# Queries and keys of the undilated pattern: from attention's projection stream to block products beside the values

## The chip, the cores and the metric

The kernel runs on one core of a Trainium2 chip. The metric is the device time of one execution in microseconds, lower is better. TensorE (PE) multiplies, VectorE (DVE) and ScalarE (ACT) do arithmetic on tiles, GpSimd (POOL) does a little arithmetic and issues some DMAs, and SyncE (SP) issues the others. Each engine works its own instructions off in order and waits at an instruction until that instruction's inputs and buffers are there.

## The reference, cut to what matters

Two residual layers on 1024 tokens of width 1024: a gated token mixer with its MLP, then attention with its MLP. Every input and weight is f32. Attention mixes three patterns (window, dilation); each has its own q, k and v for 16 heads of 64, all out of one matrix `b_w_qkv` of 1024 rows and 9 x 1024 columns.

```python
B_PATTERNS = ((128, 1), (512, 4), (2048, 16))

def mixer_b(h, w_qkv, w_out, slopes):
    B, S, _ = h.shape
    qkv = (h @ w_qkv).reshape(B, S, N_PAT, 3, B_HEADS, B_HEAD_DIM)
    outs, lses = [], []
    for g, (window, dilation) in enumerate(B_PATTERNS):
        o, lse = dilated_branch(qkv[:, :, g, 0], qkv[:, :, g, 1], qkv[:, :, g, 2],
                                window, dilation, slopes)
        outs.append(o)
        lses.append(lse)
    wts = jax.nn.softmax(jnp.stack(lses, axis=0), axis=0)[..., None]
    o = jnp.sum(wts * jnp.stack(outs, axis=0), axis=0)
    return o.reshape(B, S, B_HEADS * B_HEAD_DIM).astype(h.dtype) @ w_out
```

`dilated_branch` computes, within blocks, scaled scores plus a bias that falls with distance, a causal window mask, softmax and the weighted sum of v; it returns the log of the sum too, by which the patterns are mixed.

## The kernel before

**Split numbers.** A matrix is kept as a high part in a fast f32 format (ACT's cast, line 102) and the low rest (DVE's difference, line 103). A product is three matmuls: high by high, high by low, low by high.

**Block products.** The large matrix products of the MLPs and of v are made from half-size blocks: seven products of 512 by 512 blocks instead of eight, with sums and differences of blocks prepared beforehand. In `values` the steps are `V_STEPS`, for each pattern the products 1, 2, 5, 6, 7, 4, 3. One product is four row tiles `m` of twelve matmuls (line 1248). `RightForms` loads and prepares the weight blocks two steps ahead, `second` builds the forms of the tokens, `evict` empties an accumulator: products 1, 5 and 6 are only kept (line 1218), the others are completed (line 1222), split and stored to DRAM by a DMA that POOL issues (line 1228), from one of two buffers `vs`.

**Attention.** Work is in 24 groups, one for each of 8 head pairs and 3 patterns, in the order 2, 1, 0 of `order` (line 1312). A group has 8 slots, 4 per head, of two positions each; functions are put in slots with `at`. For tile pair `m` of a head: `scores` (two matmuls per tile, then DVE adds the bias and takes the maximum, line 1422, and ACT takes exponentials, line 1424); `transposes` one slot and a half after the scores `when` they are complete (PE into PSUM, then split by ACT and DVE); and `weighted`, one and a half slots later (PE, line 1470). POOL makes each head's bias tile (line 1404). PSUM has two banks each for scores, weighted sums, projections and transposes.

**The projection stream.** q and k of every group come from `project`, a generator: 24 groups x q and k x 2 halves x 8 steps of three matmuls (line 1344). Forty steps run ahead of slot 0 and two after each position, twelve matmuls a slot. A unit of weights is loaded one unit ahead and split (line 353, then 102 and 103); each half's accumulator is split into q or k per head, and POOL copies q's high part to the other 64 partitions (line 1354), since a score is one product over 128 rows (q high twice, against k high and low) and one with q low.

**What else is in the slots.** `load_v` loads a group's v for both heads four slots ahead. `statistics`, and in `merge` the functions `read`, `factors`, `spread`, `scale` and `add`, mix the three patterns of a head pair under the slots of the next pair; maxima, sums and factors go through DRAM. In slots 2 to 27 eight rows of the residual pass through POOL (`affine_load`, `affine_row`, lines 1596 to 1602), pinned to program order on POOL's queue. In the last group's slots the output projection (`ending`, line 389) takes the place of the stream.

**What sets the order.** The program is written in the order of the slots. A planner in the compiler may move an instruction forward on its engine where it reckons its inputs ready and its buffer free, unless `keep_in_program_order` pins it. A tile of a pool with `bufs` buffers under a tag waits until the tile that had its buffer is done with.

## Time and profile before

| | |
|---|---|
| median of 3 runs | 2761.18 us (2759.01 to 2768.53) |
| profiled execution | 2765.4 us, its span 2763.7 us |
| granted TensorE clock, mean | 0.994 |
| value stage, first to last block matmul | 999.1 to 1233.2 us |
| attention, first projection to last weighted sum | 1233.4 to 2057.9 us |
| projection matmuls in attention (line 1344) | 2304 |
| block matmuls of v (line 1248) | 1008 |

The span runs from the first to the last instruction of the profiled execution, and its own time is that of the same execution. Busy time is a union over an engine's instructions; matmuls follow each other before the one ahead has ended, so their mean duration is longer than what one adds to the total. The idle time of an engine is put down to what ended it.

### The profile page before, as it was taken

The page shows a single profiled execution, that of the slowest core. Times are in us where ns is not written, and L with a number is a line of the kernel's source. Part 1 is how long each engine was busy: PE and PEld are TensorE (multiplying, and loading weights), DVE is VectorE, ACT ScalarE, POOL GpSimd, SP SyncE. Part 2 cuts the span into 40 slices and gives each one's busy share as a digit, 9 for nine tenths or more (in the row PEclk, how much of TensorE's full clock was granted, in tenths as well). Part 3 has the DMA queues.
Part 4 walks back from the last instruction along what each step waited for, and adds up shares of the span by engine and source line. Part 5 has one row for each costly group of instructions (what it writes and reads, how often), then busy time and mean ns, then how long its engine had stood idle before and what let it go on. Part 6 is the DMA issues. An engine that isn't in the chain of part 4 may idle for free.

```text
span 2763.7 us, 36368 instructions
## 1 busy us (share of the span) xinstructions
PE 2684.8 (97%) x12954; PEld 2231.6 (81%) x12954; DVE 2022.2 (73%) x3616; ACT 1417.7 (51%) x2651; POOL 211.1 (8%) x213
## 2 busy tenths in 40 slices
PE   6999999999999999999999999999999999999998
PEld 5787787887888878888888888888877788878887
DVE  6787698787877788555677667667669965568887
ACT  3354475555443464445566665666564755544432
POOL 1001000000000001113510100111120000000000
PEclk9999999999999999999999999999999999999999
DMA  7543346667946545544533323323334564485562
GB/s 260 162 129 115 116 140 217 222 216 260 329 132 191 190 152 196 193 162 144 150 89 90 97 71 94 93 82 98 100 101 156 183 207 145 153 306 193 175 203 88
DMA packets 318187, 441.82 MB, mean 160 GB/s; under 512 B 49148, under 2 KB 174500, under 8 KB 318004
## 3 DMA queue, kind: packets, MB, share of 16 engines
q1 hardware_dynamic: 308500, 404.87, 46.3%
q0 software_dynamic: 9504, 34.61, 3.3%
q8 instruction: 102, 1.67, 0.3%
q14 instruction: 81, 0.66, 0.1%
HBM read 330.27 MB, written 109.13 MB: 159 GB/s over the span
## 4 chain that ended last, share of the span: by engine, by line
PE 69%; DVE 15%; DMA 7%; ACT 4%; issue 3%; POOL 1%; SPq 0%; DVEq 0%; ACTq 0%; POOLq 0%
PE psd L955 22%; PE psk L1344 7%; PE psua L796 7%; PE psv L1248 7%; PE psq L1344 6%; PE psuc L796 3%; DMA adaw<-in_ada_w_dram 3%; PE psd_wout L389 2%; PE pv L1470 2%; PE psu L368 2%; PE psd_wo L389 2%; PE psv L470 2%; DVE adaacc L128 2%; PE psub L796 1%; DVE left L103 1%
## 5 line engine op out<-in xcount | busy, mean ns | idle before, releaser
L796 PE MATMUL psua<-right,left 128*128 128x512 f32 x1536 | 365.8, 392 | 0.1
L955 PE MATMUL psd<-rhi,lhi 128*128 128x512 f32 x896 | 350.4, 391 | 3.0 <-ACT part L827 3.0
L955 PE MATMUL psd<-rlo,lhi 128*128 128x512 f32 x896 | 350.2, 391 | 0.2
L955 PE MATMUL psd<-rhi,llo 128*128 128x512 f32 x896 | 350.0, 391 | 0.0
L796 PEld LDWEIGHTS psua<-right,left 128*128 128x128 f32 x1536 | 288.8, 189 | 61.9 <-DVE right L103 1.0
L1424 ACT ACTIVATE p<-p,stat 128x128 f32<-128x128 f32 (+1 forms) x384 | 171.3, 446 | 168.4 <-DVE stat L1422 156.3
L955 PEld LDWEIGHTS psd<-rhi,lhi 128*128 128x128 f32 x896 | 169.0, 189 | 39.8 <-ACT part L827 3.9
L955 PEld LDWEIGHTS psd<-rlo,lhi 128*128 128x128 f32 x896 | 168.9, 188 | 35.7 <-DVE rlo L103 1.1
L955 PEld LDWEIGHTS psd<-rhi,llo 128*128 128x128 f32 x896 | 168.9, 189 | 35.2
L796 PE MATMUL psuc<-right,left 128*128 128x512 f32 x768 | 187.8, 391 | 0.0
L1344 PE MATMUL psk<-form_L,wk_hi 128*128 128x512 f32 x576 | 185.0, 402 | 0.0
L1344 PE MATMUL psq<-form_L,wq_hi 128*128 128x512 f32 x576 | 184.8, 402 | 0.0
L103 DVE TENSOR_TENSOR pTlo<-pT,pThi 128x512 fp32r<-128x512 f32 (+1 forms) x160 | 99.5, 623 | 107.9 <-ACT pThi L102 107.1
L128 DVE SCALAR_TENSOR_TENSOR adaacc<-adaw,silu_c,adaacc 128x512 f32<-128x512 f32 x168 | 132.7, 800 | 57.9 <-DMA adaw<-in_ada_w_dram 57.0
L796 PEld LDWEIGHTS psuc<-right,left 128*128 128x128 f32 x768 | 143.5, 188 | 30.1 <-DVE right L103 0.5
L103 DVE TENSOR_TENSOR left<-ws,left 128x512 fp32r<-128x512 f32 x128 | 87.8, 687 | 72.9 <-ACT left L102 71.1
L103 DVE TENSOR_TENSOR llo<-lraw,lhi 128x1024 fp32r<-128x1024 f32 x112 | 136.3, 1217 | 0.8 <-ACT lhi L102 0.8
L1422 DVE CUSTOM_DVE_ANT_0 p<-sc,bias 128x128 f32<-128x128 f32 (+1 forms) x384 | 122.5, 346 | 13.0 <-POOL bias L1404 7.6
L102 ACT CAST left<-ws 128x512 fp32r<-128x512 f32 x128 | 79.1, 620 | 98.4 <-DVE ws L717 88.3
L102 ACT CAST rhi<-rraw 128x1024 fp32r<-128x1024 f32 x48 | 50.6, 1054 | 142.9 <-issue 113.6
L1248 PE MATMUL psv<-vrhi,form_S 128*128 128x512 f32 x384 | 119.8, 390 | 1.2 <-DVE vpart L1222 0.7
L102 ACT CAST lhi<-lraw 128x1024 fp32r<-128x1024 f32 x112 | 117.3, 1047 | 3.4 <-PE psua L796 3.4
(299 smaller groups left out, 6277.6 us busy)
## 6 DMA issues: line engine op xcount, KB each, us to landing
lraw<-forms SPq DMA_DIRECT2D x112, 512.0 KB
adaw<-in_ada_w_dram SPq DMA_DIRECT2D x192, 256.0 KB
up<-in_mlp_w_up_dram SPq DMA_DIRECT2D x64, 512.0 KB
forms<-s SPq DMA_DIRECT2D x128, 256.0 KB
rraw<-in_mlp_w_down_dram SPq DMA_DIRECT2D x64, 512.0 KB
forms<-part SPq DMA_DIRECT2D x96, 256.0 KB
v<-vs POOLq DMA_DIRECT2D x48, 512.0 KB, 3.7
v<-v SPq DMA_DIRECT2D x32, 512.0 KB
```

The lines of the kernel that those rows point to most:

```text
L102: first = A.copy(hi, src) if hi_engine is A else hi_engine.tensor_copy(hi, src)
L103: return first, lo_engine.tensor_tensor(lo, src, hi, op=ALU.subtract)
L128: ins = V.scalar_tensor_tensor(acc[:], raw[:], silu_c[:, k : k + 1], acc[:], ALU.mult, ALU.add)
L368: T.matmul(dst, s[a], m[b], start=(n == 0), stop=(n == last))
L389: T.matmul(p[:], stat[a][:, k, o : o + P], u[b][:, w], start=n == 0, stop=n == count - 1)
L470: T.matmul(sums[u, half][:], units[u][a_][:, k * P : (k + 1) * P], hT[half][b_][:, k, :], start=k == 0 and a_ + b_ == 0, stop=k == KD - 1 ...
L796: T.matmul(acc, w[:, a, k, :], right[p][:, b, k, :], start=p in (1, 2, 5) and k + a + b == 0, stop=k == 3 and a == 1, skip_group_check=True)
L955: ins = T.matmul(sums[kind, m][:], l[a][:, k, m * P : (m + 1) * P], r[b][:, k, :], start=p in (1, 5, 2, 3) and kp + k + a + b == 0, stop=k ...
L1248: T.matmul(acc, left[:, a, 2 * kp + k, m * P : (m + 1) * P], r[b][:, k, :], start=p in (1, 2, 5) and kp + k + a + b == 0, stop=kp == 1 and ...
L1344: T.matmul(p[:], wu[a][:, k * P : (k + 1) * P], h_op(k, half, b), start=k + c_ == 0, stop=k == KD - 1 and c_ == 2)
L1422: V.tensor_tensor_reduce(out=pr[:, 0:w], in0=scb[:, sl], in1=st["bias"][:, width - w :], scale=-0.125, scalar=3e38, op0=ALU.add, op1=ALU.m ...
L1424: A.activation(pr[:, 0:w], pr[:, 0:w], AF.Exp, bias=nm, scale=-1.0, accum_out=l)
```

## The change

q and k of pattern 0 leave the projection stream. They become two more matrices of the block products, ahead of the three of v: `V_BLOCKS` names thirds of patterns (0 and 1 are q and k of pattern 0, then v of 0, 2 and 1). For them the weights' columns are the stationary side and the tokens the moving side, so that the result comes out with columns on the partitions; it is split, and each tile goes to `qk_dram` by two DMAs, one per head. Before a group of pattern 0, `load_qk` brings q (high part twice), k (high, low) and q's low part into buffers of the weights' tags; one weight buffer `raw_u` is left for the stream's loads.

The groups run in the order 0, 2, 1. The stream has 512 steps instead of 768, and `due` says how many shall be issued by each position: 14 at the start, 70 at slot 16, 92 at slot 24, then evenly to 512 two slots before the last group, which is eight matmuls a slot. Transposes come one slot later and weighted sums one and a half (with a floor); three fixed buffer pairs hold the transposed probabilities; v is loaded per head, in the slot where its head begins; the merge's functions move by half a slot to a slot, with another order of patterns; loads of the output stage move by up to two slots, and its last two rows are loaded singly.

```diff
+    qk_dram = [dram.tile([2 * N_PAIRS, 2, HEAD, S], F32, name=f"{n}_0") for n in "qk"]
...
-            r0, c0 = row * HALF + kp * 2 * P, g * 3 * D + 2 * D + col * HALF
+            r0, c0 = row * HALF + kp * 2 * P, of * D + col * HALF
...
+    V_BLOCKS = (0, 1, 2, 8, 5)
+    V_STEPS = [(of, p) for of in V_BLOCKS for p in (1, 2, 5, 6, 7, 4, 3)]
...
                 half, dh = {2: (1, 0), 3: (1, 1), 4: (0, 0), 7: (0, 1)}[p]
...
+                w = parted.tile([P, 2 * HALF], F32R, name=f"vs_{of}_{p}_{m}", tag="vs")
+                if of % 3 == 2:
+                    v = w[:].rearrange("p (h f c) -> p h f c", f=4, c=HEAD)
+                    split(v[:, :, 0:4:3, :], v[:, :, 1:3, :], acc.rearrange("p (h e c) -> p h e c", e=2, c=HEAD))
+                    i = 4 * half + m
+                    nc.gpsimd.dma_start(v_dram[of // 3][i * P : (i + 1) * P, 4 * dh : 4 * dh + 4, :],
+                                        v.rearrange("p h f c -> p h (f c)").bitcast(F32))
+                else:
+                    parts_ = w[:].rearrange("p (s n) -> p s n", s=2)
+                    split(parts_[:, 0, :], parts_[:, 1, :], acc)
+                    for e in range(2):
+                        head = qk_dram[of][2 * (4 * dh + m) + e].rearrange("s c t -> c s t")
+                        nc.gpsimd.dma_start(head[:, :, half * HALF : (half + 1) * HALF],
+                                            parts_[64 * e : 64 * e + 64].bitcast(F32))
...
-                                T.matmul(acc, left[:, a, 2 * kp + k, m * P : (m + 1) * P], r[b][:, k, :],
-                                         start=p in (1, 2, 5) and kp + k + a + b == 0,
+                                tokens, columns = left[:, a, 2 * kp + k, :], r[b][:, k, :]
+                                if of % 3 == 2:
+                                    stat, mov = tokens[:, m * P : (m + 1) * P], columns
+                                else:
+                                    stat, mov = columns[:, m * P : (m + 1) * P], tokens
+                                T.matmul(acc, stat, mov, start=p in (1, 2, 5) and kp + k + a + b == 0,
                                          stop=kp == 1 and k == 1 and a == 1, skip_group_check=True)
...
+            dist = work.tile([P, HALF], F32, name="dist", tag="h")
+            near, far = dist[:, 0 : 2 * P], dist[:, 2 * P : 3 * P]
...
+            raw_u, zlo = (wts.tile([P, D], F32R if n else F32, name=("w_raw", "zlo_0")[n], tag="raw", bufs=2) for n in range(2))
+            zlo = [zlo, ql.tile([P, S], F32R, name="zlo_1", tag="zlo")]
+            for t in zlo:
+                V.memset(t[64:P, :].bitcast(F32), 0.0)
...
+            pT_bufs = [tuple(where.tile([P, HALF], F32R, name=f"pT{m}_{n}", tag="h" if where is work else f"pT{m}{n}", bufs=2 if where is work else 1)
+                             for m, where in (("hi", qp if n else work), ("lo", qp))) for n in range(3)]
+            n_pT = 0
...
-            order = [(hp, g) for hp in range(N_PAIRS) for g in (2, 1, 0)]
+            order = [(hp, g) for hp in range(N_PAIRS) for g in (0, 2, 1)]
...
-                todo = [(n, X) for n in range(len(order)) for X in range(2)]
+                todo = [(n, X) for n in range(len(order)) if order[n][1] for X in range(2)]
...
-                    return unit(b_w_qkv[0, :, c0 : c0 + P], f"w{'qk'[X]}_{hp}_{g}")
+                    return unit(b_w_qkv[0, :, c0 : c0 + P], f"w{'qk'[X]}_{hp}_{g}", raw=raw_u[:])
...
-                for n, X, half in [(n, X, half) for n, X in todo for half in (1, 0)]:
+                yield True
+                for i, n, X, half in [(i, n, X, half) for i, (n, X) in enumerate(todo) for half in (1, 0)]:
...
+            def load_qk(n):
+                hp = order[n][0]
+                q, k = ([wts.tile([P, S], F32R, name=f"{nm}{e}_{hp}_0", tag=tag) for e in range(2)] for nm, tag in (("q", "whi"), ("k", "wlo")))
+                for e in range(2):
+                    rows = [d[2 * hp + e].rearrange("s c t -> (s c) t") for d in qk_dram]
+                    nc.sync.dma_start(k[e][:].bitcast(F32), rows[1])
+                    for i in range(2):
+                        nc.sync.dma_start(q[e][64 * i : 64 * i + 64, :].bitcast(F32), rows[0][0:64])
+                    nc.sync.dma_start(zlo[e][0:64, :].bitcast(F32), rows[0][64:P])
+                got[n].update(q0=q[0], q1=q[1], k0=k[0], k1=k[1], qlo=zlo)
...
-                @at(max(base - 4, 0), 0)
...
+                def load_v(e):
+
+                    my[f"v{e}"] = qp.tile([P, NT, 2 * HEAD], F32R, name=f"v{e}_{hp}_{g}", tag="v")
+                    dst = my[f"v{e}"][:].bitcast(F32)
+                    src = v_dram[g][:, hp, 2 * e * HEAD : 2 * (e + 1) * HEAD]
...
+                if g == 0:
+                    if n:
+                        at(base - 6, 0)(lambda: load_qk(n))
+                for e in range(2):
+                    at(base + 4 * e, 0)(lambda e=e: load_v(e))
...
-                        hi = work.tile([P, HALF], F32R, name=f"pThi_{h}_{g}_{m}", tag="h")
-                        lo = qp.tile([P, HALF], F32R, name=f"pTlo_{h}_{g}_{m}", tag="pTlo")
+                        nonlocal n_pT
+                        hi, lo = pT_bufs[n_pT % 3]
+                        n_pT += 1
...
-                        at(base + 4 * e + w + 1, 1)(lambda m=m, f=transposes: f(m))
-                        at(base + 4 * e + w + 3, 0)(lambda m=m, f=weighted: f(m))
+                        at(base + 4 * e + w + 2, 1)(lambda m=m, f=transposes: f(m))
+                        at(base + 4 * e + max(w, 1) + 4, 1)(lambda m=m, f=weighted: f(m))
...
-                @at(base + 3, 0)
+                @at(base + 3, 1)
...
-                @at(base + 3, 1)
+                @at(base + 4, 0)
                 def spread():
-                    for g in (1, 2, 0):
-                        bc = box[g] = row_bc(f"bc_{hp}_{g}")
+                    for g in (2, 1, 0):
+                        box[g] = row_bc(f"bc_{hp}_{g}")
+                    for g in (0, 2, 1):
                         for e in range(2):
-                            nc.sync.dma_start(bc[64 * e : 64 * e + 64, :], w_dram[hp, g, e].partition_broadcast(64))
+                            nc.sync.dma_start(box[g][64 * e : 64 * e + 64, :], w_dram[hp, g, e].partition_broadcast(64))
...
-                steps = [lambda f=f, g=g, half=half: f(g, half) for f, g in ((scale, 2), (scale, 1), (scale, 0), (add, 2), (add, 1)) for half in range(2)]
+                steps = [lambda f=f, g=g, half=half: f(g, half) for f, g in ((scale, 0), (scale, 2), (add, 2), (scale, 1), (add, 1)) for half in range(2)]
...
-                    n = pace * n + 12 if hp < N_PAIRS - 1 else n // 2 + 10
+                    n = pace * n + 14 if hp < N_PAIRS - 1 else n // 2 + 10
...
-            staged_unit(0, (-8, 0), (-6, 0), (-5, 0))
+            staged_unit(0, (-10, 0), (-6, 1), (-5, 1))
             staged_unit(1, (-8, 1), (-5, 1), (-4, 1))
             staged_unit(2, (-4, 0), (-3, 0), (-2, 0))
-            staged_unit(3, (-3, 0), (-2, 1), (-1, 1))
+            staged_unit(3, (-3, 1), (-2, 0), (-1, 0))
...
+            due = ((0, 14), (16, 70), (24, 92), (last_group - 2, 512))
...
             stream = project()
-            for _ in range(5 * KD):
-                next(stream)
+            next(stream)
+            load_qk(0)
+            done = 0
...
+                for pos, fs in enumerate(slot):
+                    for f in fs:
                         f()
-                    if not all([next(stream, None) for _ in range(2)]) and n >= last_group:
+                    while done < due_at(n + (pos + 1) / 2):
+                        next(stream)
+                        done += 1
+                    if n >= last_group:
                         if "begin" not in ending:
+                            assert next(stream, None) is None
                             output()
                         next(ending["begin"], None)
```

The parts left out rename `g` to `of`, use the new tiles in place of the old, move `gate_row` by one slot, and load the last rows with `load_o4` and `load_o5`.

More of the change, by code (lines that the diff above doesn't have):

```diff
@@ L1336, in project @@
                         if nm == "q":
-                            got[n]["qlo"] = [qlo[e][n % 2] for e in range(2)]
+                            got[n]["qlo"] = [qlo[e][g - 1] for e in range(2)]
                         for m in ((f"{nm}0", f"{nm}1")):
@@ L1355, in project @@
                         yield True
+            def load_qk(n):
[8 more added lines that the diff above has]
+                got[n].update(q0=q[0], q1=q[1], k0=k[0], k1=k[1], qlo=zlo)
             def row_bc(name):
                 return work.tile([P, S], F32, name=name, tag="res", bufs=3)
-            slots = [[[], []] for _ in range(8 * len(order) + 10)]
+            slots = [[[], []] for _ in range(8 * len(order) + 12)]
             def at(slot, pos):
@@ L1403, in scores @@
                             st["bias"] = qp.tile([P, width], F32, name=f"bias_{h}_{g}", tag="bias")
[L1404 removed]
+                            G.tensor_scalar(st["bias"][:], far if g == 2 else near,
                                             -8.0 * DILATION[g] * 2.0 ** (-8.0 * (h + 1) / N_HEADS), 1.0, ALU.mult, ALU.mult)
```

103 lines of the change are left out of this document (48 added, 55 removed).

## The prediction

> **What bounds the kernel now.** The first part of the page gives the engines' shares, the second the span in slices.
>
> ```profile
> span 2763.7 us, 36368 instructions
> ...
> PE 2684.8 (97%) x12954; PEld 2231.6 (81%) x12954; DVE 2022.2 (73%) x3616; ACT 1417.7 (51%) x2651; POOL 211.1 (8%) x213
> ...
> PE   6999999999999999999999999999999999999998
> ...
> PEclk9999999999999999999999999999999999999999
> ```
>
> TensorE is busy nearly everywhere at a full clock. A busy PE need not be at its peak, so I looked next at busy time by stretch. The columns are length, then busy time and instructions of PE, PEld, DVE, ACT and POOL, clock, DMA share and GB/s. The rows are the head of attention (projections alone), three consecutive groups of steady attention (patterns 2, 1, 0 of one head pair), the three together, the end of attention, and the value stage.
>
> ```profile
> 1233.00:1260.50 27.50, 27.50 (x123) 22.78 (x122) 13.46 (x17) 9.91 (x14) 4.27 (x7) 1.00 0.68 210
> 1556.30:1588.30 32.00, 32.00 (x188) 27.76 (x187) 21.48 (x66) 18.73 (x51) 3.38 (x4) 1.00 0.43 118
> 1588.30:1622.40 34.10, 32.56 (x187) 27.57 (x186) 25.27 (x62) 20.45 (x57) 3.38 (x4) 1.00 0.25 74
> 1622.40:1654.70 32.30, 32.30 (x187) 27.91 (x187) 21.13 (x54) 21.38 (x54) 3.17 (x4) 1.00 0.30 72
> 1556.30:1654.70 98.40, 96.86 (x557) 83.24 (x557) 67.88 (x181) 60.55 (x160) 9.93 (x12) 1.00 0.33 88
> 1989.00:2060.00 71.00, 63.65 (x343) 53.53 (x342) 55.53 (x115) 45.84 (x117) 23.52 (x12) 0.93 0.37 120
> 999.00:1233.00 234.00, 232.80 (x1040) 191.57 (x1040) 162.24 (x212) 109.31 (x158) 27.91 (x50) 1.00 0.53 187
> ```
>
> The value stage idles 1.2 us on PE, a steady head pair 98.40 - 96.86 = 1.54 us. DVE has the most to do behind PE: 67.88 of 98.40 us, 69%. Both stages that the change touches are bound by PE's issue. What one projection matmul costs there is read in the chain of waits (start, length, what):
>
> ```profile
> 1244.47 10.88 PE psk L1344 x48
> ...
> 1569.29 2.78 PE psk L1344 x12
> ```
>
> That is 10.88 / 48 = 0.227 us where projections follow each other, and 2.78 / 12 = 0.232 us in bursts of twelve between attention matmuls (a single matmul's 0.39 us in the groups overlaps its neighbours). In the value stage 32 transposes take 4.1 us, the row below, so a block matmul costs (234.0 - 4.1) / 1008 = 0.228 us, its idle included.
>
> ```profile
> L1248 PE MATMUL psv<-vrhi,form_S 128*128 128x512 f32 x383 | 119.4, 390 | 1.2 <-DVE vpart L1222 0.7 <-ACT vrhi L102 0.5
> ...
> L1155 PE MATMUL pst<-ident,acc 128*128 128x128 f32 x32 | 4.1, 272 | 0.0
> ```
>
> **Matmuls removed and added.** q and k of pattern 0 cost 8 head pairs x 2 x 2 halves x 24 = 768 matmuls in attention. As block products they are 2 x 7 products x 4 x 12 = 672. Of the 120 ahead of the slots 48 stay, so 72 go at 0.227 (16.3 us) and 696 at 0.232 (161.5 us): -177.8 us. Added: 672 x 0.228 = +153.2 us. **Net -24.6 us.** Swapping the stationary and the moving side leaves 128 by 128 by 512.
>
> **Other engines in attention.** Per pair go two weight preparations, eight evictions (cast and difference) and two copies of q on POOL:
>
> ```profile
> L103 DVE TENSOR_TENSOR qlo<-psq,q 64x512 fp32r<-64x512 f32 x86 | 59.1, 687 | 22.5 <-ACT q L102 21.9
> ...
> L1354 POOL TENSOR_SCALAR q<-q 64x1024 fp32r<-64x1024 f32 x44 | 54.1, 1230 | 206.9 <-ACT q L102 206.4
> L102 ACT CAST q<-psq 64x512 fp32r<-64x512 f32 x85 | 49.2, 579 | 35.4 <-DVE qlo L103 29.6 <-PE psq L1344 5.0 <-POOL aff L1601 0.7
> ...
> L103 DVE TENSOR_TENSOR wq_lo<-wq_raw,wq_hi 128x1024 fp32r<-128x1024 f32 x19 | 23.3, 1225 | 33.5 <-ACT wq_hi L102 33.5
> ...
> L102 ACT CAST wq_hi<-wq_raw 128x1024 fp32r<-128x1024 f32 x19 | 19.9, 1048 | 7.5 <-PE psq L1344 7.4
> ```
>
> DVE loses 8 x 0.687 + 2 x 1.225 = 7.9, ACT 8 x 0.579 + 2 x 1.048 = 6.7 us. A pair falls to 98.4 - 96 x 0.232 = 76.1 us; DVE's 60.0 us are then 79% of it, ACT's 53.8 71%. PE stays the bound on average, but less evenly: the merge, six products and four sums, 6 x 0.949 + 4 x 0.723 = 8.6 us of DVE by the rows below, now lies under the slots of pattern 2.
>
> ```profile
> L1560 DVE TENSOR_TENSOR bc<-oT,bc 128x512 f32<-128x512 f32 x42 | 39.9, 949 | 3.1 <-DMA bc<-w_dram 2.6
> ...
> L1564 DVE TENSOR_TENSOR bc<-bc,bc 128x512 f32<-128x512 f32 x28 | 20.2, 723 | 0.3
> ```
>
> The waits tell how near the next limit is.
>
> ```profile
> DVE pTlo L103 <- ACT pThi L102: 107.1, 102, 1.7
> ...
> PEld pT L1450 <- ACT p L1424: 16.1, 18, 1.9
> ...
> DVE p L1422 <- POOL bias L1404: 7.6, 2, 4.5
> ```
>
> PE's recurrent stall is a transpose waiting for its exponentials, in the group whose DVE is busiest (25.27 of 34.10 us, 74%). The change gives that wait 2.5 slots of 3.2 us, 7.9 us, where it had 1.5 of 4.1, 6.2 us; transposes to weighted sums get 2 slots, 6.3 us, for 1.5, 6.2 us. More room, fuller DVE. If all idle time of steady pairs goes, that is -8 x 1.5 = -12 us. If DVE cannot pass the 74% of its busiest group, a pair takes 60.0 / 0.74 = 81.1 us, +5.0, or +40 us over eight. I take 0: more room and more load pull opposite ways.
>
> **The first slots and POOL's queue.** Eight rows of the residual go through POOL, pinned in order: load, two products, store.
>
> ```profile
> 1272.74 0.54 POOL L1596 DMA_DIRECT2D aff<-spill  x1
> ...
> 1376.86 2.40 POOL L1601 TENSOR_TENSOR aff<-aff,aff_b 128x1024 f32<-128x1024 f32 x1
> 1379.34 0.29 POOL L1404 TENSOR_SCALAR bias<-far 128x128 f32<-128x128 f32 x1
> ```
>
> From the first load to the bias behind the last product is 106.6 us, spread over slots 2 to 28. DVE waited there for a bias, as the waits say (7.6 us), and PE for DVE. The chain consists of landings and POOL's own products and doesn't shrink; the slots do. Up to slot 16 a slot has 10.5 projection matmuls, 98.4 / 24 - 1.5 x 0.232 = 3.75 us, then 8.25 and 8 (3.2 us): slots 2 to 28 take 14 x 3.75 + 12 x 3.2 = 90.9 us. The same bias would be 15.7 us late; two score banks (two slots, 6.4 us) hide part. Bounds 0 (the planner moves the bias forward) and +15.7; I take +6, since some stall is in the trace already.
>
> **Stores of q and k.** A value tile leaves by one POOL DMA, a q or k tile by two, each from 64 partitions. The page's DMA issues (size, us to landing), the value stage's groups and its waits:
>
> ```profile
> v<-vs POOLq DMA_DIRECT2D x48, 512.0 KB, 3.7
> ```
>
> ```profile
> L1228 POOL DMA_DIRECT2D v<-vs x45 | 24.2, 538 | 895.2 <-DVE vs L103 894.1 <-DVE far L1283 1.1
> L103 DVE TENSOR_TENSOR vs<-vpart,vs 128x512 fp32r<-128x512 f32 x34 | 23.6, 694 | 16.4 <-ACT vs L102 16.3
> ...
> L102 ACT CAST vs<-vpart 128x512 fp32r<-128x512 f32 x34 | 21.1, 621 | 56.5 <-DVE vpart L1222 26.3 <-DMA v<-vs 23.1 <-DVE vraw L1108 3.6
> ```
>
> ```profile
> ACT vs L102 <- DMA v<-vs: 40.9, 18, 5.0
> ```
>
> With two buffers and a tile every 12 x 0.228 = 2.74 us, a buffer has 5.5 us; cast, difference, issue and landing are 0.6 + 0.7 + 0.5 + 3.7 = 5.5, and ACT did wait 40.9 us in the value stage. It cost PE at most its 1.2 us there. Were the two halves to land one after the other, a buffer would take 5.5 + 0.5 + 3.7 = 9.7 us, 4.9 per tile: over twelve tiles in a row 26 us late, less one product without stores (10.9 us), 15 us a block, +30. Below, 0. I take +2: the same bytes on the same queue, nearest the measured row. [...]
>
> **The seam.** Slot 0 is now pattern 0, and its scores wait for k, q and the low part of q from DRAM (1.25 MB for the first head), into weight buffers that the last block product frees. At the 210 GB/s of the head of attention that is 6.2 us, with one landing of 3.7 us 9.9. Sixteen projection steps (48 x 0.227 = 10.9 us) can cover it if the planner issues them first; if not, PE waits with everything behind the first score. Bounds 0 and +9.9; I take +2. Later loads of q and k are issued six slots, 19 us, ahead: eight SP issues per pair against two weight loads taken away, plus five more for v in halves. A value load now waits on SP for the head before it and goes out 5.5 slots, 17 us, ahead of use; what queues behind it there (weights, statistics, factors) has two slots or more. Nothing of this is on the path while landings stay near 3.7 us; doubled, they still fit. The swapped roles of the last pattern's statistics and the reordered output stage I cost at 0; the end of attention idles 71.00 - 63.65 = 7.4 us and hides or loses a few (+-4).
>
> **Sum.** -24.6 + 0 + 6 + 2 + 2 = -14.6 us. The profiled execution took 2765.4 us (span 2763.7, 1.7 around it): 2750.8. It lies 4.2 above the median of the three runs, so the forecast is 2761.2 - 14.6 = **2747 us**.
>
> **Rivals.**
>
> - **All the gain.** The longer lags remove the steady stalls and POOL's lateness is planned around: 2761.2 - 24.6 - 12 = 2725. For: stalls come from one wait that gets 1.7 us more. Against: DVE from 69 to 79%.
> - **POOL's chain decides.** The bias is late by its bound: 2747 + 9.7 = 2757, within the noise. For: the chain's 106.6 us don't shrink. Against: a bias needs no input but its buffer.
> - **DVE becomes the bound (slower).** Place: the slots of patterns 2 and 0. DVE blocks in order on ACT's casts (107.1 us of waits), so it may not be fillable beyond 74%. Price +40: 2787. It decides once a pair exceeds 76.1 + 14.6 / 8 = 77.9 us, DVE's ceiling at 60.0 / 77.9 = 77%. Against: 74% was no ceiling, PE set that group's length but for 1.54 us.
> - **The stores serialize**: 2747 + 28 = 2775. Against: 40.9 us of the same waits were hidden.
> - **The clock.** The end of attention, with PE 90% busy, ran at 0.93. At 0.93 throughout, some 8 x 76 = 608 us would take 608 x (1 / 0.93 - 1) = 46 us more: 2793. Against: steady attention, as mixed, shows 1.00. [...]
>
> That the change saves no matmuls can be excluded: 672 and 768 are counted.
>
> **How the numbers follow.** Chances: forecast 0.51, all the gain 0.16, POOL 0.16, DVE 0.11, stores 0.04, clock 0.02. The range, 2728 to 2766, leaves out the last three and the lowest end of the second; the likeliest's own is 2736 to 2756. About 0.3% (8.3 us) can be told from no change. Faster means under 2752.9: 0.46 of the forecast, 0.16 and 0.03 of POOL's, 0.65. Slower, over 2769.5: 0.11 + 0.04 + 0.02 = 0.17. The rest, 0.18.
>
> **What would show it.** The block stage near 234 + 153 + 2 = 389 us with PE idle of a few us; a steady pair near 76 us with DVE near 79%; 1536 projection matmuls left. A bias wait of DVE well above 7.6 us speaks for POOL's chain, PE waiting for differences or exponentials in every pair for DVE, PE idle at block ends behind ACT's store waits for the stores. The forecast is wrong if a steady pair is above 77.9 or the block stage above 400 us.

## The result and the profile after

The changed kernel takes 2781.72 us (median; 2781.12 to 2789.98), the kernel before 2760.59 us beside it: a ratio of 1.0078, 95% interval 1.0051 to 1.0105. It is **slower by 21 us** (0.8%), where 14 us of gain were forecast, and it lies above the range.

The page of the changed kernel, shares and slices:

```profile
span 2779.4 us, 36657 instructions
...
PE 2668.7 (96%) x12858; PEld 2222.1 (80%) x12858; DVE 2036.6 (73%) x3638; ACT 1419.5 (51%) x2655; POOL 238.3 (9%) x261
...
PE   6999999999999999999997999999988999999998
PEclk9999999999999999999998999999999999999999
```

TensorE has 16 us less to do than before (2668.7 for 2684.8) and the span is 15.7 us longer: the saved work is there, and about twice as much was lost in waiting (PE's idle time grew from 78.9 to 110.7 us). The slices show where: a 7 in the 22nd (about 1460 to 1530 us) and two 8s around the end of attention (about 2020 to 2150). So the next view is busy time by stretch. The rows are the block stage, the eight head pairs (first score to first score; the last to its last weighted sum), and all that follows:

```profile
995.10:1383.20 388.10, 386.20 (x1715) 318.23 (x1714) 252.74 (x318) 170.76 (x244) 68.02 (x115) 1.00 0.58 189
1390.50:1480.50 90.00, 87.77 (x498) 76.00 (x499) 52.88 (x150) 55.08 (x148) 41.70 (x34) 0.98 0.62 186
1480.50:1574.70 94.20, 79.26 (x460) 68.92 (x459) 59.05 (x167) 52.23 (x149) 25.98 (x24) 0.91 0.49 136
1574.70:1652.20 77.50, 75.00 (x460) 65.68 (x459) 58.81 (x176) 52.65 (x150) 8.46 (x10) 1.00 0.53 131
1652.20:1730.50 78.30, 75.20 (x460) 65.57 (x459) 58.30 (x173) 53.03 (x152) 8.47 (x10) 1.00 0.52 130
1730.50:1808.50 78.00, 75.20 (x461) 65.70 (x460) 57.71 (x168) 52.36 (x148) 8.93 (x10) 1.00 0.51 131
1808.50:1891.90 83.40, 78.26 (x458) 67.40 (x457) 58.03 (x173) 52.55 (x149) 6.95 (x10) 0.96 0.48 122
1891.90:1970.20 78.30, 75.38 (x460) 65.56 (x459) 58.71 (x174) 52.75 (x151) 7.71 (x10) 1.00 0.50 130
1970.20:2069.20 99.00, 87.89 (x498) 74.83 (x496) 75.11 (x186) 65.18 (x175) 22.19 (x14) 0.94 0.50 140
2069.20:2779.40 710.20, 688.95 (x3045) 566.23 (x3044) 540.71 (x794) 339.11 (x501) 4.04 (x2) 0.99 0.53 178
```

The same view of the kernel before: its first two pairs, pairs 3 to 7 together, the last pair, and what follows.

```profile
1260.60:1356.70 96.10, 94.56 (x534) 80.99 (x533) 58.75 (x153) 58.28 (x153) 46.78 (x38) 1.00 0.44 133
1356.70:1458.10 101.40, 98.08 (x558) 83.36 (x557) 68.54 (x182) 61.55 (x164) 21.06 (x20) 1.00 0.38 106
1458.10:1949.30 491.20, 484.43 (x2778) 416.53 (x2777) 339.50 (x905) 302.47 (x796) 49.65 (x60) 1.00 0.33 88
1949.30:2058.20 108.90, 100.86 (x556) 85.15 (x555) 79.72 (x189) 65.30 (x175) 27.16 (x16) 0.95 0.36 108
2058.20:2763.70 705.50, 688.35 (x3044) 564.79 (x3043) 536.24 (x794) 337.71 (x501) 0.00 (x0) 0.99 0.54 179
```

From these rows the loss can be placed. In the changed kernel 100 projections fewer lie ahead of the first score (20 for 120), 35 fewer in the first pair, 96 in each of the next six, 57 in the last. At the prediction's 0.232 us the pairs should take what stands in the second column:

| stretch | should take | took | lost |
|---|---|---|---|
| first pair | 96.1 - 8.1 = 88.0 | 90.0 | 2.0 |
| second pair | 101.4 - 22.3 = 79.1 | 94.2 | 15.1 |
| pairs 3 to 7 | 491.2 - 111.4 = 379.8 | 395.5 | 15.7 |
| last pair | 108.9 - 13.2 = 95.7 | 99.0 | 3.3 |
| after attention | 705.5 | 710.2 | 4.7 |

With the block stage (388.1 - 234.0 = +154.1) and the seam (+2.4: 7.3 us for 27.6, with 100 projections at 0.227 us fewer), -177.8 + 154.1 + 2.4 + 40.8 = +19.5 us. The spans differ by 15.7, and the profiled execution of before entered its block stage 3.9 us late (999.0 for 995.1): together 19.6.

In the first two pairs it is POOL. Its timeline in the changed kernel (start, length, line; in brackets the idle time before and what ended it):

```profile
1471.83 0.40 POOL L1443 TENSOR_SCALAR bias<-dist 128x256 f32<-128x256 f32 x1
...
1488.99 0.54 POOL L1637 DMA_DIRECT2D aff<-spill  x1 [4.94 <-DMA spill<-aff]
1492.49 2.33 POOL L1642 TENSOR_TENSOR aff<-aff,aff_g 128x1024 f32<-128x1024 f32 x1 [2.96 <-DMA aff<-spill]
1494.91 2.33 POOL L1642 TENSOR_TENSOR aff<-aff,aff_b 128x1024 f32<-128x1024 f32 x1
1497.65 0.59 POOL L1643 DMA_DIRECT2D spill<-aff  x1 [0.41 <-POOL aff L1642]
1498.27 0.42 POOL L1443 TENSOR_SCALAR bias<-dist 128x256 f32<-128x256 f32 x1
```

The bias of the second pair's first head stands behind the seventh row, and within that row POOL waits 4.94 us for the last store, then 2.96 for the load. The pair's scores began at 1480.5; the bias came at 1498.3. The waits of the whole execution say the same (engine, who waited for whom: us, times, longest):

```profile
DVE p L1461 <- POOL bias L1443: 20.2, 2, 15.9
DVE pTlo L103 <- ACT pThi L102: 30.7, 36, 2.0
```

DVE lost 15.9 us at one bias (4.5 before). The second row was 107.1 us before: with the longer lags and fuller engines DVE seldom arrives before ACT any more. PE's wait for exponentials (16.1 us before) is gone from the list.

What such a gap costs beyond itself is seen in windows of 5 us around it, and in two windows around a shorter gap in the sixth pair:

```profile
1485.00:1490.00 5.00, 2.34 (x15) 1.73 (x13) 0.00 (x0) 0.00 (x0) 0.54 (x1) 1.00 0.60 188
1490.00:1495.00 5.00, 0.00 (x0) 0.00 (x0) 0.00 (x0) 0.00 (x0) 2.42 (x2) 0.65 0.31 105
1495.00:1500.00 5.00, 0.58 (x2) 0.59 (x3) 0.64 (x4) 0.89 (x4) 4.29 (x4) 0.50 0.25 102
1500.00:1505.00 5.00, 5.00 (x18) 4.42 (x18) 4.45 (x8) 4.43 (x12) 1.77 (x3) 0.50 0.33 111
1505.00:1510.00 5.00, 5.00 (x31) 4.29 (x31) 3.84 (x12) 3.08 (x10) 4.64 (x2) 0.99 0.83 241
...
1826.00:1829.40 3.40, 1.30 (x8) 0.98 (x8) 3.17 (x20) 2.54 (x8) 0.00 (x0) 1.00 0.48 145
1829.40:1836.20 6.80, 6.03 (x21) 5.29 (x22) 3.59 (x11) 3.36 (x11) 0.00 (x0) 0.50 0.54 110
```

After the long gap the granted clock is 0.50 until about 1505 us, and 18 matmuls pass in a window that holds 31 at full clock. In the sixth pair PE waited 2.4 us at one transpose and was busy for 1.30 of 3.4 us; the clock is 0.50 for the 6.8 us that follow, in which 21 matmuls pass, where the next 3.4 us hold 22. So this gap cost about 3 us more than itself. The sixth pair takes 83.4 us and its neighbours 78: about three of these five us are busy time (78.3 us for 75.3), two are waiting.

### The profile page after: what moved, and what is told of

It reads as the page before. It is cut to its first block, busy times and chain, and to the rows that moved or that the text cites. A ratio compares the mean times of both kernels' runs of the same rounds, so it can differ in the third digit from the quotient of the medians.

```text
span 2779.4 us, 36657 instructions
## 1 busy us (share of the span) xinstructions
PE 2668.7 (96%) x12858; PEld 2222.1 (80%) x12858; DVE 2036.6 (73%) x3638; ACT 1419.5 (51%) x2655; POOL 238.3 (9%) x261
## 4 chain that ended last, share of the span: by engine, by line
PE 68%; DVE 14%; DMA 7%; ACT 5%; issue 3%; POOL 2%; SPq 0%; DVEq 0%; ACTq 0%; POOLq 0%
PE psd L955 21%; PE psv L1265 10%; PE psua L796 8%; PE psuc L796 4%; PE psu L368 3%; PE psq L1366 3%; PE psk L1366 3%; PE psd_wout L389 2%; PE psd_wo L389 2%; DMA adaw<-in_ada_w_dram 2%; PE psv L470 2%; PE psub L796 2%; PE pv L1510 2%; ACT p L1463 1%; POOL aff L1642 1%
## 5 line engine op out<-in xcount | busy, mean ns | idle before, releaser
L1461 DVE CUSTOM_DVE_ANT_0 p<-sc,bias 128x128 f32<-128x128 f32 (+1 forms) x384 | 119.0, 343 | 29.4 <-POOL bias L1443 20.2
L102 ACT CAST left<-ws 128x512 fp32r<-128x512 f32 x128 | 79.1, 620 | 96.5 <-DVE ws L717 86.6
L1366 PE MATMUL psk<-form_L,wk_hi 128*128 128x512 f32 x384 | 126.7, 411 | 0.0
L1366 PE MATMUL psq<-form_L,wq_hi 128*128 128x512 f32 x384 | 126.0, 410 | 0.0
L103 DVE TENSOR_TENSOR pTlo<-pT,pThi 128x384 fp32r<-128x384 f32 (+1 forms) x160 | 98.4, 620 | 32.1 <-ACT pThi L102 30.7
L1520 DVE TENSOR_TENSOR oT<-oT,pv 64x512 f32<-64x512 f32 x96 | 65.8, 685 | 74.9 <-ACT oT L1519 74.1
```

The lines of the kernel that those rows point to most:

```text
L102: first = A.copy(hi, src) if hi_engine is A else hi_engine.tensor_copy(hi, src)
L103: return first, lo_engine.tensor_tensor(lo, src, hi, op=ALU.subtract)
L1366: T.matmul(p[:], wu[a][:, k * P : (k + 1) * P], h_op(k, half, b), start=k + c_ == 0, stop=k == KD - 1 and c_ == 2)
L1461: V.tensor_tensor_reduce(out=pr[:, 0:w], in0=scb[:, sl], in1=st["bias"][:, width - w :], scale=-0.125, scalar=3e38, op0=ALU.add, op1=ALU.m ...
L1520: V.tensor_tensor(dst, dst, pvs[b][main, :], op=ALU.add)
```

## Experiments

The theory: the loss is POOL's chain of residual rows (first two pairs) and DVE, too full in the slots of patterns 0 and 2 (the pairs after). The rivals: that PSUM's transpose banks, the lags or the clock by itself make the later pairs long, and that only the bias behind POOL's queue makes the second pair long. The changed kernel's number for pairs 3 to 7 is 395.5 us throughout. Totals are compared by their ratios to the kernel before (0.001 is 2.76 us), the medians' difference stands beside them; between two such ratios some 9 us either way are uncertain, so smaller things are read from the stretches of the traces. Each trace is of one execution. The stretch ahead of the block stage, in which the runs of the changed kernel do not differ, took from 992 to 1001 us in them; this much noise is in the totals.

### Without the residual rows, after and before

```diff
-                at(2 + 3 * i, 0)(lambda i=i: affine_load(i))
-                at(3 + 3 * i, 1)(lambda i=i: affine_row(i))
+                pass
```

> The changed kernel without the eight residual rows that go through POOL (load, two products, store; they are left out of the computation). Theory POOL: the bias of the second head pair stands behind the last product on POOL, and PE's waits of 12.5, 2.6 and 2.2 us there and the low clock after them come from that: time falls by 15 to 22 us, to about 2763 (ratio to before 1.001), the second pair takes about 78 us in place of 94.2, DVE's wait for a bias falls from 20.2 us to a few. Rival DVE/PSUM: the loss is in every pair, from DVE's work; then the second pair falls by no more than 5 us. If the clock alone made the second pair long, it stays above 85 us with few waits.

> The kernel before without the same eight rows (left out of the computation): the control. Theory POOL: DVE waited 7.6 us for a bias there, of which PE lost a part; time falls by 3 to 8 us, to about 2755 (ratio 0.998). What the changed kernel gains more than this by the same omission is what the change made of POOL's chain. Rival: if both fall by the same, the chain is not where the change lost its gain.

Measured: 2758.37 us, ratio 0.9979 (0.9962 to 0.9996), without the rows; 2756.48, 0.9961 (0.9949 to 0.9974), for the kernel before without them. The omission is worth 27 us after (1.0078 - 0.9979; 23 by the medians) and 11 us before (7 by the medians, 2763.71 beside them), both above what was expected. Either way **the change made 16 us of the rows' cost**, give or take 9. The traces agree: without the rows the first two pairs are 22.3 us shorter after and 5.2 before, a difference of 17.1, which is the table's 2.0 + 15.1. DVE's wait for a bias falls from 20.2 us to 1.5. The second pair and pairs 3 to 7 of the changed kernel without rows:

```profile
1477.10:1553.20 76.10, 74.89 (x461) 65.72 (x460) 57.68 (x167) 51.41 (x145) 8.21 (x9) 1.00 0.53 134
1553.20:1946.20 393.00, 377.65 (x2293) 328.81 (x2292) 291.44 (x859) 263.38 (x746) 41.73 (x50) 1.00 0.50 129
```

The second pair falls to 76.1 us, the pair length of the prediction; the later ones hardly move. Without rows the change is still worth nothing (2758.4 against 2756.5): the other half of the loss is elsewhere.

### The bias on ACT

```diff
-                            G.tensor_scalar(st["bias"][:], far if g == 2 else near,
-                                            -8.0 * DILATION[g] * 2.0 ** (-8.0 * (h + 1) / N_HEADS), 1.0, ALU.mult, ALU.mult)
+                            A.activation(st["bias"][:], far if g == 2 else near, AF.Copy,
+                                         scale=-8.0 * DILATION[g] * 2.0 ** (-8.0 * (h + 1) / N_HEADS))
```

> The changed kernel with the six bias tiles of a head pair made by ACT in place of POOL, so that POOL's rows stay and nothing waits behind them. Theory POOL (a bias behind the queue): gain 12 to 20 us as without the rows, less what 6 x 0.3 us on ACT cost per pair; about 2765 (1.002). [...]

Measured: 2780.91 us, 1.007 (1.0043 to 1.0096). By the total the theory in this form fell: the gain is 0.8 us by the medians, 2 by the ratios. The trace says why: the second pair did shrink to 86.4 us, not to 78, because the next in the queue took the bias's place, and pairs 3 to 7 grew to 399.9 with 7.8 us more on ACT (that this is the reason isn't shown). DVE and POOL in that run:

```profile
1512.53 0.69 DVE L1601 TENSOR_TENSOR bc<-oT,bc 128x512 f32<-128x512 f32 x1 [4.17 <-POOL q L1376]
```

```profile
1507.98 2.40 POOL L1642 TENSOR_TENSOR aff<-aff,aff_b 128x1024 f32<-128x1024 f32 x1
...
1511.45 1.04 POOL L1376 TENSOR_SCALAR q<-q 64x1024 fp32r<-64x1024 f32 x1
```

The first product of the merge waits 4.17 us on DVE, with scores and transposes queued behind it, until a copy of q is done that stands behind the last row. The merge's tiles also take their buffers from the same three (`res`) as the rows. So it isn't one instruction that is late: the chain as a whole is too long for slots that have become shorter. DVE and POOL did hold each other up in this run (last section): two of DVE's operations took 1.20 and 1.83 us for 0.17 each, 2.7 us too long together; that is too little for the loss.

### The rows spread out

Four rows in slots 2 to 20, two in slots 42 to 49, two in slots 66 to 73, between the merges that need the buffers.

```diff
-                if i == 0:
+                if i in (0, 4, 6):
...
-            for i in range(NT):
-                at(2 + 3 * i, 0)(lambda i=i: affine_load(i))
-                at(3 + 3 * i, 1)(lambda i=i: affine_row(i))
+            for i, s in enumerate((2, 7, 12, 17, 42, 46, 66, 70)):
+                at(s, 0)(lambda i=i: affine_load(i))
+                at(s + (3 if i in (0, 4, 6) else 2), 1)(lambda i=i: affine_row(i))
```

> The changed kernel with the eight residual rows spread out: four in slots 2 to 20, two in slots 42 to 49, two in slots 66 to 73 (with the two row vectors loaded again), so that the row buffers are free when the first merge takes them and no other POOL instruction stands behind a whole chain. Nothing is left out. Theory, the chain as a resource (POOL's queue and the row buffers together): the second pair falls from 94.2 us to 78 to 80, total by 12 to 20 us, to about 2765 (ratio 1.000 to 1.003). Rival, POOL's rows cost wherever they stand: the later pairs with rows grow by as much, total within 5 us of the changed kernel's.

Measured: 2764.89 us, 0.9999 (0.9983 to 1.0015): 22 us better by the ratio, 17 by the medians, as the theory said. The second pair:

```profile
1479.50:1555.70 76.20, 74.87 (x461) 65.69 (x460) 57.61 (x167) 51.38 (x145) 14.50 (x16) 1.00 0.60 161
```

Pairs 3 to 7 take 399.3 us, 3.8 more, where four of the rows now stand; the third pair alone takes 82.4 for 77.5, at a granted clock of 0.96. The rows are cheaper there, not free.

### Pattern 0's last transposes half a slot later

```diff
-                        at(base + 4 * e + w + 2, 1)(lambda m=m, f=transposes: f(m))
+                        late = g == 0 and m == 3
+                        at(base + 4 * e + w + 2 + late, 0 if late else 1)(lambda m=m, f=transposes: f(m))
```

> The changed kernel with the last transposes of pattern 0 half a slot later, so that two pairs of transposes of one slot no longer follow each other into the two banks. Theory PSUM bank: the gap of 1.6 to 1.9 us that recurs once per head pair (PE's transposes waiting for DVE's low part of pT) goes, 8 x 1.7 = about -13 us, to 2769 (1.003); a steady pair falls from 78 to 76.4. Rival, DVE is too full: the gap moves to the next wait for DVE, the pair stays at 77.5 to 78.3 and the time within 3 us of the changed kernel's.

Measured: 2782.23 us, 1.0066 (1.0045 to 1.0088), the same as the changed kernel within the interval. Pairs 3 to 7 take 390.4, 5 us less, of which 3 in the sixth (80.3 for 83.4), where the clock stayed at 1.00 in this run; 3.7 went back into the second pair, 97.9 for 94.2. PE's waits in the fourth and fifth pair, first of the changed kernel, then of this one (pT: the transposes of the probabilities; pv: the weighted sums; pstat: the transpose of the statistics; pTlo: the low part of the transposed probabilities):

```profile
PE pT L1486 <- DVE pTlo L103: 3.0, 2, 1.5
PE pv L1510 <- DVE pTlo L103: 1.4, 3, 0.5
PE pstat L1534 <- DVE pTlo L103: 1.0, 1, 1.0
```

```profile
PE pv L1510 <- DVE pTlo L103: 1.5, 3, 0.5
PE pT L1486 <- DVE pTlo L103: 1.4, 2, 0.7
PE pstat L1535 <- DVE pTlo L103: 1.0, 1, 1.0
```

The transposes' wait shrinks by half with the same work on DVE and does not go: where they stand decides a part of it. The banks are the place where PE meets the lateness, and DVE, which makes the low part of pT, is what is late.

### The merge left out, and moved

The merge's sums and four of its six products left out:

```diff
+                def skip(g, half):
+                    pass
...
-                    in_order(V.tensor_tensor(box[0][:, w], box[0][:, w], box[g][:, w], op=ALU.add))
...
-                steps = [lambda f=f, g=g, half=half: f(g, half) for f, g in ((scale, 0), (scale, 2), (add, 2), (scale, 1), (add, 1)) for half in range(2)]
+                steps = [lambda f=f, g=g, half=half: f(g, half) for f, g in ((scale, 0), (skip, 2), (skip, 2), (skip, 1), (add, 1)) for half in range(2)]
```

> The changed kernel without most of the merge of the three patterns (two products of six and none of the four sums are left in a pair; the output lacks two patterns): DVE has 6.4 us less to do per pair, under pattern 2 and at the end of pattern 0. Theory, DVE full in the slots of patterns 0 and 2: the wait of pstat and weighted sums for the low part of pT in pattern 2 goes (0.9 to 1.7 us per pair), that of the transposes in pattern 0 (1.4 to 1.9) stays or shrinks by half, since pattern 0 carries only the merge's first two products; steady pair 76.3 to 77.0 in place of 77.5 to 78.3. Rival, the two transpose banks of PSUM: both waits stay as they are.

Measured: 2756.72 us (one time). Pairs 3 to 7:

```profile
1573.60:1956.10 382.50, 374.06 (x2293) 328.78 (x2292) 260.55 (x815) 264.99 (x750) 40.97 (x51) 1.00 0.53 133
```

31.0 us less on DVE (291.6 to 260.6) make the pairs 13.0 us shorter, 76.5 a pair. Over these pairs PE's waits for weighted sums and statistics fall from 6.6 us to 0.8, as the theory said. The transposes' wait stays, 7.6 us for 8.0. Then without leaving anything out: the sums (but for the last pair) and the merge's nine small operations on POOL.

```diff
-                        V.tensor_tensor(a[:, g], m[:], nm[:, g], op=ALU.subtract)
+                        G.tensor_tensor(a[:, g], m[:], nm[:, g], op=ALU.subtract)
...
-                    in_order(V.tensor_tensor(box[0][:, w], box[0][:, w], box[g][:, w], op=ALU.add))
+                    in_order((G if hp < N_PAIRS - 1 else V).tensor_tensor(box[0][:, w], box[0][:, w], box[g][:, w], op=ALU.add))
```

> The changed kernel with the merge's four sums per pair (but for the last pair) and its nine small sums, differences and products of 16 and 48 columns made by POOL in place of DVE; the rows of the residual stay as they are. Nothing is left out. DVE has 2.7 + 1.9 = 4.6 us less to do in a pair, of which 1.9 in pattern 0's slots. Theory, DVE full: the waits for the low part of pT shrink, pairs 3 to 7 take 76.3 to 77.3 us in place of 77.5 to 78.4 (and 83.4), total 6 to 12 us below the changed kernel, about 2772 (1.004). Rival, that the waits are PSUM's two transpose banks or the order: pairs stay at 77.5 to 78.4, total within 3 us.

Measured: 2775.33 us, 1.0045 (1.003 to 1.0061), 9 us better by the ratio, 6 by the medians. The trace doesn't bear this total out: attention as a whole took 678.9 us in it, and 678.8 in the changed kernel, because the first pair took 97.5 for 90.0. Its rows were late there once more, and PE waited 4.7 us at one score. Pairs 3 to 7 fall by 5.4 us for 16.7 us less on DVE:

```profile
1577.80:1967.90 390.10, 377.08 (x2295) 328.73 (x2294) 274.91 (x794) 263.40 (x750) 78.25 (x116) 1.00 0.51 130
```

Beside each other, pairs 3 to 7 of one execution each, in us (clock: granted, in the sixth pair; the last two columns are waits of PE for DVE):

| run | pairs 3 to 7 | DVE busy | sixth pair | clock | pT | pv and pstat |
|---|---|---|---|---|---|---|
| changed kernel | 395.5 | 291.6 | 83.4 | 0.96 | 8.0 | 6.6 |
| without rows | 393.0 | 291.4 | 81.6 | 0.98 | 8.0 | 5.9 |
| transposes later | 390.4 | 290.2 | 80.3 | 1.00 | 4.5 | 7.6 |
| most of the merge left out | 382.5 | 260.6 | 77.8 | 0.98 | 7.6 | 0.8 |
| sums and small operations on POOL | 390.1 | 274.9 | 79.7 | 0.98 | 7.6 | 3.6 |

A microsecond taken off DVE, busy 74% of the time in the changed kernel (291.6 of 395.5), gave 0.42 and 0.32 us in the last two rows. Some of that is the sixth pair's clock: 0.04 of 83.4 us are 3.3 us, 0.02 in the last two rows 1.6. Without this difference the two prices are 0.37 and 0.23. The second rests on few us, since the second and third row differ from the first by 2.5 and 5.1 us with DVE's work as it was. What is shown is that the merge's work on DVE holds up the weighted sums and the statistics. The transposes' wait, most of it in pattern 0, did not answer to it. In the sixth pair of the changed kernel DVE works almost without a pause from 1824.8 us until the low part that PE waits for: a weighted sum's result, scores, a low part of q, and the merge's small operations, which the run without most of the merge keeps. With these on POOL, DVE waits for POOL instead, 1.38 us at the same place, and PE's gap is 2.6 us.

### Weight low parts on POOL

```diff
-                    return unit(b_w_qkv[0, :, c0 : c0 + P], f"w{'qk'[X]}_{hp}_{g}", raw=raw_u[:])
+                    return unit(b_w_qkv[0, :, c0 : c0 + P], f"w{'qk'[X]}_{hp}_{g}", raw=raw_u[:],
+                                lo_engine=G if hp >= 2 else V)
```

> The changed kernel with the low parts of the projection weights made by POOL in place of DVE from the third head pair on: four subtractions of 1.22 us a pair, two of them in pattern 0's slots, leave DVE (58.8 to 53.9 us a pair). Nothing is left out. Theory DVE: the recurring waits for the low part of pT shrink from 2.5 to 3.1 us a pair to about 1, pairs 3 to 7 take 76 to 76.8 us and the total falls by 7 to 12 us, to about 2771. Rival PSUM banks: the gap of 1.6 to 1.9 in pattern 0 stays, total within 3 us.

Measured: 2800.37 us, 1.0136 (1.011 to 1.0162): 16 to 19 us worse than the changed kernel, though DVE had 17.7 us less to do in pairs 3 to 7. Neither theory had this. In the fourth pair POOL's difference (2.40 us; DVE takes 1.22) ends at 1670.36, and only then can the next weights be loaded into the one buffer `raw_u`. POOL and ACT of that run:

```profile
1667.96 2.40 POOL L103 TENSOR_TENSOR wk_lo<-w_raw,wk_hi 128x1024 fp32r<-128x1024 f32 x1 [4.39 <-ACT wk_hi L102]
```

```profile
1674.09 1.05 ACT L102 CAST wq_hi<-w_raw 128x1024 fp32r<-128x1024 f32 x1 [1.18 <-DMA w_raw<-in_b_w_qkv_dram]
```

ACT stands 1.18 us at the weights, with its exponentials, evictions and casts of pT behind it, and 5 us later PE waits 3.5 us. The same cast waits 0.16 us in the changed kernel at this place; the change had given the second raw buffer to the low part of q. That this chain explains all of the loss isn't shown; the clock, 0.96 over these pairs (0.99 in the changed kernel), has a part in it. The run decides nothing on DVE's load.

### The lags of before

```diff
-                        at(base + 4 * e + w + 2, 1)(lambda m=m, f=transposes: f(m))
-                        at(base + 4 * e + max(w, 1) + 4, 1)(lambda m=m, f=weighted: f(m))
+                        at(base + 4 * e + w + 1, 1)(lambda m=m, f=transposes: f(m))
+                        at(base + 4 * e + w + 3, 0)(lambda m=m, f=weighted: f(m))
```

> The changed kernel with the lags of before: transposes and weighted sums half a slot to a slot earlier behind their scores (1.5 slots and 3 in place of 2.5 and 5). Theory, the longer lags did remove the wait for the exponentials: it comes back at 1.4 us or more per group with full DVE, steady pairs grow from 78 to 80 to 84 us. Rival, the lags are beside the point and DVE's load sets the pair: 77.5 to 78.5 as now.

Measured: 2778.98 us (one time). Pairs 3 to 7 take 399.5 us, 79.9 a pair (78.5 to 81.6), between the two expectations (of the lags, the weighted sums' is 4.5 slots in the changed kernel by the diff, not 5); the last pair takes 94.3 for 99.0. In this one execution the longer lags are worth about 4 us in the steady pairs, and cost 5 in the last, where there are fewer projections to fill the wait. On balance next to nothing of the 21 us lies here.

### The repairs together

The edits of the three sections on the spread rows, on the merge on POOL and on the transposes, put together; in the last kernel this besides:

```diff
+                        if hp == N_PAIRS - 1:
+                            at(base + 4 * e + w + 1, 1)(lambda m=m, f=transposes: f(m))
+                            at(base + 4 * e + w + 3, 0)(lambda m=m, f=weighted: f(m))
+                            continue
```

> Both repairs together: the residual rows spread out (17 us in the run of that alone) and the merge's sums and small operations on POOL. Nothing is left out. If the two causes are separate, their gains add: 17 + 6 to 12, about 2754 (ratio 0.995 to 0.998), faster than the kernel before. If POOL's queue is the common cause, the rows and the merge's sums stand in each other's way in pairs 2 and 3 and the time stays at 2762 to 2766.

> The same with the last transposes of pattern 0 half a slot later. With DVE relieved, the wait that is left at that place (1.2 to 2.2 us a pair in the run without most of the merge, gone into pstat's wait in the run of the shift alone) should now go: 76.1 us a pair, 3 to 8 us less than without the shift, about 2748 (0.993). If DVE is still full there, no difference (within 3 us).

> The three repairs (rows spread out, merge's sums and small operations on POOL, last transposes of pattern 0 half a slot later) and, in the last head pair alone, the lags of before. Nothing is left out. Theory, that with few projections left to fill it the last pair pays for the longer lags (99.1 us in the changed kernel, 94.3 in the run with the lags of before, where the weighted sums had 3.2 us of wait less): the last pair falls by 3 to 5 us, total to about 2752 (0.996). Rival, that its time goes to the merge behind the last weighted sums: what the pair gains is waited for there, no difference within 2 us.

| kernel | median us | ratio | pairs 3 to 7 | last pair |
|---|---|---|---|---|
| rows spread, merge on POOL | 2758.45 | 0.9983 (0.9971 to 0.9994) | 392.7 | 98.4 |
| and transposes later | 2756.11 | 0.9977 (0.9966 to 0.9988) | 390.1 | 99.0 |
| and the last pair's old lags | 2752.00 | 0.9958 (0.9940 to 0.9977) | 390.0 | 95.0 |

The gains add, as far as can be told: 22 and 9 us alone, 26 together by the ratios (17, 6 and 23 by the medians). Pairs 3 to 7 are 6.6 us shorter than with the rows spread alone (399.3). The shift of the transposes adds less than the intervals can tell. The last pair gives 4.0 us and the median falls by 4.1. The last kernel is faster than both: 0.42% under the kernel before, where the forecast had 0.5% for the change alone. The kernel before was not run with the same repairs; without its rows it took 2756.48 us, so how much of the change's saving is in the last kernel isn't shown. Its second pair and its last:

```profile
1475.90:1552.50 76.60, 75.07 (x461) 65.52 (x460) 54.33 (x154) 51.11 (x145) 23.17 (x29) 1.00 0.64 167
1942.50:2037.50 95.00, 88.81 (x498) 76.16 (x497) 70.36 (x172) 63.97 (x171) 26.33 (x25) 0.93 0.50 138
```

## Why the prediction was wrong, by its own steps

- **Matmuls, -24.6: right.** The block stage took +154.1 for the +153.2 predicted (20 projections, not 48, came ahead of the first score, at much the same price). PE's busy time fell by 16.1 us in all. In pairs 3 to 7 it is 379.0 us, where 484.4 - 111.4 = 373.0 were due: 3 of these 6 us are the lowered clock of the sixth pair (0.96). The other pairs ran at 1.00 and were busy for 75.0 to 75.4 us where 74.6 were due, as if a projection had cost 0.227 us there too and not 0.232; no run decides that.
- **Stores of q and k, +2: right**, at most 0.9 with everything else in that stage. The rival that they serialize to a price fell. The issues of the block stage (size, us to landing) show that half a tile lands no sooner than a whole one, and that it was hidden all the same:

```profile
v<-vs POOLq DMA_DIRECT2D x46, 512.0 KB, 3.2
q<-vs POOLq DMA_DIRECT2D x32, 256.0 KB, 4.6
```

The second half of a tile of q is issued 0.6 us behind the first and lands 1.3 us behind it (median): held up by 0.7 us, where the rival had a whole landing of 3.7.

- **The seam, +2: right**, 2.4.
- **POOL's chain, +6: the first step that failed.** The runs show +16 to 17, over its upper bound (15.7). The idea of the bound was right: the chain did not shrink (108.1 us from the first load to the bias behind the last product, 106.6 before), and a bias came 16 us late. But it was another bias than the one that the bound was worked out for, the first head's behind the seventh row, so that 15.9 lies so near 15.7 is luck. The choice of 6 was wrong, in two places. "Two score banks (two slots, 6.4 us) hide part": PE stood still from about 1487.3 to 1499.4 us, 12 us of DVE's wait of 15.9. And the price went beyond the wait: after the gap PE ran at a clock of 0.50 until about 1505 us, and other users of POOL and of the row buffers came late too, as the run with the bias on ACT shows.
- **Steady pairs, 0: the second step that failed.** It was +15.7 over pairs 3 to 7. Both sides of "more room and more load pull opposite ways" were there, but not of one size: the waits for exponentials went, and waits for DVE came; PE's idle time rose from 1.4 us a pair (491.2 - 484.4 over five) to 3.3 (395.5 - 379.0 over five), and the lowered clock behind the longest of them (0.50 for 6.8 us) took about 3 us more in all. The prediction had the right rival, with 77.9 us as the point at which DVE decides: the pairs took 77.5 to 78.3, and one 83.4. Its ceiling of 74%, priced at +5.0 a pair, was near for DVE's load (58.3 us of 78.3) and dismissed because PE had set the length before. It was neither a ceiling nor one slope: with the merge's work off DVE the waits of weighted sums and statistics went, and the transposes' wait in pattern 0 stayed, since the instructions ahead of its low part are others.
- **End of attention, 0 (4 either way): mis-sized.** +3.3 in the last pair and +4.7 behind it. The longer lags made the first (with the old lags the last pair takes 95.0 for 99.0). The stretch behind it, span less end of the last pair, takes 708.3 to 712.5 us in the eleven traces of changed kernels with the whole merge, and 704.5 and 705.5 in the two of the kernel before. So some 3 to 8 us are the change's, and which of its edits made them stays open. In the run without most of the merge it takes 2755.0 - 2048.8 = 706.2 us, in one execution, too near the others to tie it to the merge.
- **The clock**, a rival with 0.02, came in, not as 0.93 throughout, as priced (the mean was 0.988, and 0.994 before), but as a surcharge on gaps: 0.50 behind the two that the windows show.

The forecast failed because three terms with bounds on both sides all came out slower than they were taken. Two of them, POOL's chain and the steady pairs, share a cause: less time per slot for the engines that aren't the bound.

## What to carry to other kernels

When the bound engine gets less to do per slot, list every chain that is paced by something else (a queue of loads, products and stores; a single buffer; an engine as busy as DVE here, 74% of pairs 3 to 7) and ask whether it still fits into the shorter slots; here that was worth more than the saved matmuls. Take the instruction that is late for a symptom: moved away, its successor in the queue was late instead, and only a shorter or spread-out chain helped. Work taken off the second-busiest engine gives back something only where the bound engine waits behind that very work: here 0.2 to 0.4 us per microsecond over the pairs, and nothing at the transposes' wait.

## What the runs showed of the hardware

**Some gaps of TensorE cost more than their length here, and one did not.** After 12 us without work the clock was granted at 0.50 for nearly 6 us of work, and after 2.4 us for the next 6.8 (the windows above). At the same place in the sixth pair, after a wait of 2.4 to 2.6 us, it was lowered for 3.4 us only in the run without rows and in the two runs with less of the merge on DVE. In the run with the weights' low parts on POOL a wait of 3.5 us left it at 1.00:

```profile
1677.70:1681.10 3.40, 1.80 (x12) 1.30 (x10) 3.18 (x17) 2.31 (x8) 0.00 (x0) 1.00 0.53 154
1681.10:1684.50 3.40, 1.48 (x10) 1.39 (x11) 2.84 (x9) 2.49 (x7) 0.00 (x0) 1.00 0.23 45
```

The lowered stretches in attention last 3.4, 6.8, 10.2 or 13.7 us in the changed kernel's trace. In the windows of 3.4 us that are shown, the wait of 3.5 us falls into two, with PE busy for 1.80 and 1.48 us; that of 2.4 us falls into one, with 1.30. So the length of a gap alone didn't decide: one of 2.4 us cost three more and one of 3.5 us none. What lowers the clock isn't shown.

**DVE and POOL held each other up in some operations on tiles in SBUF.** In the run with the bias on ACT two DVE minima over 16 columns, 0.17 us in the median of the changed kernel, took 1.20 and 1.83 us while POOL's products ran. One of these products took 3.03 us for its usual 2.40; it began under a difference of DVE between two tiles in SBUF (1492.01, 1.23 us):

```profile
1494.33 1.20 DVE L1567 TENSOR_TENSOR mm<-mst 128x16 f32<-128x16 f32 x1
...
1496.17 1.83 DVE L1568 TENSOR_TENSOR mm<-mm,mst 128x16 f32<-128x16 f32 x1
```

```profile
1492.47 3.03 POOL L1642 TENSOR_TENSOR aff<-aff,aff_g 128x1024 f32<-128x1024 f32 x1 [3.04 <-DMA aff<-spill]
1495.58 2.39 POOL L1642 TENSOR_TENSOR aff<-aff,aff_b 128x1024 f32<-128x1024 f32 x1
```

Both minima end where a product ends (1495.5, 1498.0). DVE's low parts of q, read out of PSUM, show no such delay: in the first two pairs of the changed kernel they took 687 ns with no product of POOL beside them and 690 ns where a product overlapped them (means of 15 and 5).
